# Rotary embedding over 16 heads: all rows on VectorE and GpSimd in groups of three, the first tile loaded ahead of the tables

## The chip, the cores and the metric

The kernel runs on one core of one Trainium2 chip. A core has TensorE (matrix multiply, writes to PSUM), VectorE (called DVE in the profile), ScalarE (ACT), GpSimd (POOL) and SyncE (SP), which here only issues transfers. Data is moved between the chip's memory and the on-chip SBUF by 16 DMA engines. The metric is the device time of one execution in microseconds (us), taken as the median of several runs.

## The reference

The input x is 16 x 512 x 1024 float32: batch, position, and 16 heads of 64 numbers. Each head's numbers are taken as two halves x1 and x2 of 32, and rotated with a cosine and a sine that depend on the position and on the place within the half:

```python
x = x.reshape(batch, seq, num_heads, head_dim)
x1, x2 = x[..., :half_dim], x[..., half_dim:]
cos, sin = cos[None, :, None, :], sin[None, :, None, :]
rotated = np.concatenate([x1 * cos - x2 * sin, x1 * sin + x2 * cos], axis=-1)
```

All is float32. x has 33.6 MB and so has the output: 67.1 MB must be moved. The tables cos and sin are 512 x 32 each, 64 KB.

## The kernel before, in words

**Tiling.** Two batch elements make one tile: 128 partitions, of which each holds R = 8 consecutive positions ("rows" of 1024 numbers), 32 KB a partition and 4 MB in all. There are NT = 8 tiles and NB = 5 buffers for them (pool `xin`). A tile is worked on in place and stored from where it was loaded.

**Tables.** The 64 partitions of `tabs` hold sin and cos once. A selection matrix `sel` (from `ident`, L75 to L83) and three matmuls (L88 to L90) spread them over 128 partitions in PSUM: `cos_ps`, and `sns_ps`, in which -sin and +sin lie side by side. ScalarE copies `sns_ps` to `sns` in SBUF (L94), since GpSimd reads it there. It also copies `cos_ps` to `cost` (L95), which nothing reads.

**Work on a tile** (`compute`). The output is x * cos + swap(x) * sns, where swap exchanges the halves of each head. The view `swapped` does the exchange in the access pattern, `cosb` and `snsb` repeat a table over the heads. Eight rows are divided in two ways:

- Rows 0 and 1 (`PEROWS`): the product swap(x) * sns is made by GpSimd for row 0 and by VectorE for row 1 (L121, tile `B`); VectorE multiplies x by cos in place (L131); TensorE adds the two by multiplying both with the identity into one PSUM tile `ps` (L136, L137, in halves of 512); ScalarE copies the sum back (L138).
- Rows 2 to 7 in three pairs (`PAIRS`): GpSimd makes T = swap(x) * sns (L126), VectorE makes pp = x * cos in PSUM (L142) and adds T and pp into x (L143).

`T` has two buffers, `pp` one. So GpSimd can be at most two groups ahead of VectorE.

**Order.** It is written out by hand (`manual_schedule`): each engine runs its instructions in the order of the program text. All transfers are issued by SP, in this order: sin, cos, the first tile in two halves (L63, L64), the loads of tiles 1 to 4 (L68), the stores of tiles 0 to 2 as each is done (L148), the loads of tiles 5 to 7, which each wait until a buffer has been stored (L68), the stores of tiles 3 and 4 (L152), of tiles 5 and 6 (L156), and tile 7 in two halves (L157, L158). A transfer that waits holds up those behind it on SP.

Of the kernel before, what the change touches and what calls it, by code (L numbers as in the profile page):

```python
# [7 lines left out]
FP32 = mybir.dt.float32  # L8
ALU = mybir.AluOpType


@with_exitstack
def kernel(
    ctx: ExitStack,
    tc: tile.TileContext,
    x: bass.AP,
    cos: bass.AP,
    sin: bass.AP,
    num_heads: bass.AP,
    out: bass.AP,  # L20
):
    nc = tc.nc
    P = nc.NUM_PARTITIONS
    batch, seq, dim = x.shape
    nh = num_heads
    hd = dim // nh
    half = hd // 2


    BP = 2  # L30
    HP = P // BP
    R = seq // HP
    NT = batch // BP
    assert HP * R == seq and BP * NT == batch
    NB = 5
    PAIRS = (2, 4, 6)
    PEROWS = (0, 1)

    xv = x.rearrange("b (p r) d -> (b p) (r d)", r=R)
    xv = xv.rearrange("(t p) f -> t p f", p=P)  # L40
    ov = out.rearrange("b (p r) h d -> (b p) (r h d)", r=R)
    ov = ov.rearrange("(t p) f -> t p f", p=P)
    cosv = cos.rearrange("(p r) j -> p (r j)", r=R)
    sinv = sin.rearrange("(p r) j -> p (r j)", r=R)

    fixed = ctx.enter_context(tc.tile_pool(name="fixed", bufs=1))
    xin = ctx.enter_context(tc.tile_pool(name="xin", bufs=NB))
    tpool = ctx.enter_context(tc.tile_pool(name="tpool", bufs=2))
    bpool = ctx.enter_context(tc.tile_pool(name="bpool", bufs=2))
    ptab = ctx.enter_context(tc.tile_pool(name="ptab", bufs=1, space=bass.MemoryType.PSUM))  # L50
    ppair = ctx.enter_context(tc.tile_pool(name="ppair", bufs=1, space=bass.MemoryType.PSUM))
    prow = ctx.enter_context(tc.tile_pool(name="prow", bufs=2, space=bass.MemoryType.PSUM))

    ctx.enter_context(tc.manual_schedule())


    tabs = fixed.tile([HP, 2, R * half], FP32, name="tabs")
    x_tiles = [None] * NT
    x_tiles[0] = xin.tile([P, R * dim], FP32, name="x_sb")
    H = R * dim // 2  # L60
    nc.sync.dma_start(out=tabs[:, 1], in_=sinv)
    nc.sync.dma_start(out=tabs[:, 0], in_=cosv)
    nc.sync.dma_start(out=x_tiles[0][:, :H], in_=xv[0][:, :H])  # L63
    nc.sync.dma_start(out=x_tiles[0][:, H:], in_=xv[0][:, H:])  # L64

    def load(t):
        x_tiles[t] = xin.tile([P, R * dim], FP32, name="x_sb")
        nc.sync.dma_start(out=x_tiles[t], in_=xv[t])  # L68

    for t in range(1, NB):  # L70
        load(t)


    ident = fixed.tile([P, P], FP32, name="ident")
    nc.gpsimd.memset(ident, 0.0)  # L75
    nc.gpsimd.affine_select(  # L76
        out=ident, in_=ident, compare_op=ALU.not_equal, fill=1.0,
        base=0, pattern=[[-1, P]], channel_multiplier=1,
    )
    sel = fixed.tile([HP, 2, P], FP32, name="sel")  # L80
    nc.vector.tensor_copy(out=sel[:, 0, :HP], in_=ident[:HP, :HP])  # L81
    nc.vector.tensor_copy(out=sel[:, 0, HP:], in_=ident[:HP, :HP])
    nc.vector.tensor_scalar_mul(out=sel[:, 1, :], in0=sel[:, 0, :], scalar1=-1.0)  # L83

    sns_ps = ptab.tile([P, R, 2, half], FP32, name="sns_ps")
    cos_ps = ptab.tile([P, R, half], FP32, name="cos_ps")
    sin3 = tabs[:, 1].rearrange("p (r j) -> p r j", r=R)
    nc.tensor.matmul(out=sns_ps[:, :, 1, :], lhsT=sel[:, 0, :], rhs=sin3, start=True, stop=True)  # L88
    nc.tensor.matmul(out=sns_ps[:, :, 0, :], lhsT=sel[:, 1, :], rhs=sin3, start=True, stop=True)  # L89
    nc.tensor.matmul(out=cos_ps.rearrange("p r j -> p (r j)"), lhsT=sel[:, 0, :], rhs=tabs[:, 0],  # L90
                     start=True, stop=True)
    sns = fixed.tile([P, R, 2, half], FP32, name="sns")
    cost = fixed.tile([P, R, half], FP32, name="cost")
    nc.scalar.copy(out=sns, in_=sns_ps)  # L94
    nc.scalar.copy(out=cost, in_=cos_ps)  # L95

    def view(ap, r0, n):

        return ap[:, r0 * dim:(r0 + n) * dim]

    def cosb(tab, r0, n):
        return bass.AP(tensor=tab.tensor, offset=tab.offset + r0 * half,
                       ap=[tab.ap[0], [half, n], [0, 2 * nh], [1, half]])

    def snsb(tab, r0, n):
        return bass.AP(tensor=tab.tensor, offset=tab.offset + r0 * hd,
                       ap=[tab.ap[0], [hd, n], [0, nh], [1, hd]])

    def swapped(xt, r0, n):
        return bass.AP(tensor=xt.tensor, offset=xt.offset + r0 * dim + half,  # L110
                       ap=[xt.ap[0], [hd, n * nh], [-half, 2], [1, half]])

    def compute(t):
        xt = x_tiles[t]
        ts = {}
        bs = {}

        for r in PEROWS:
            B = bpool.tile([P, dim], FP32, name="B")
            eng = nc.vector if r == PEROWS[-1] else nc.gpsimd  # L120
            eng.tensor_tensor(out=B, in0=swapped(xt, r, 1), in1=snsb(sns_ps if eng is nc.vector else sns, r, 1),  # L121
                              op=ALU.mult)
            bs[r] = B
        for r0 in PAIRS:
            T = tpool.tile([P, 2 * dim], FP32, name="T")
            nc.gpsimd.tensor_tensor(out=T, in0=swapped(xt, r0, 2), in1=snsb(sns, r0, 2), op=ALU.mult)  # L126
            ts[r0] = T

        for r in reversed(PEROWS):
            xr = view(xt, r, 1)  # L130
            nc.vector.tensor_tensor(out=xr, in0=xr, in1=cosb(cos_ps, r, 1), op=ALU.mult)  # L131
            for c in range(2):
                ps = prow.tile([P, dim // 2], FP32, name="ps")
                xc = xr[:, c * dim // 2:(c + 1) * dim // 2]
                bc = bs[r][:, c * dim // 2:(c + 1) * dim // 2]
                nc.tensor.matmul(out=ps, lhsT=ident, rhs=xc, start=True, stop=False)  # L136
                nc.tensor.matmul(out=ps, lhsT=ident, rhs=bc, start=False, stop=True)  # L137
                nc.scalar.copy(out=xc, in_=ps)  # L138
        for r0 in PAIRS:
            pp = ppair.tile([P, 2 * dim], FP32, name="pp")  # L140
            xr = view(xt, r0, 2)
            nc.vector.tensor_tensor(out=pp, in0=xr, in1=cosb(cos_ps, r0, 2), op=ALU.mult)  # L142
            nc.vector.tensor_tensor(out=xr, in0=ts[r0], in1=pp, op=ALU.add)  # L143

    for t in range(NB):
        compute(t)
        if t < NT - NB:
            nc.sync.dma_start(out=ov[t], in_=x_tiles[t])  # L148
    for t in range(NB, NT):
        load(t)  # L150
    for t in range(NT - NB, NB):
        nc.sync.dma_start(out=ov[t], in_=x_tiles[t])  # L152
    for t in range(NB, NT):
        compute(t)
        if t < NT - 1:
            nc.sync.dma_start(out=ov[t], in_=x_tiles[t])  # L156
    nc.sync.dma_start(out=ov[NT - 1][:, :H], in_=x_tiles[NT - 1][:, :H])  # L157
    nc.sync.dma_start(out=ov[NT - 1][:, H:], in_=x_tiles[NT - 1][:, H:])  # L158


# [33 lines left out]
```

## Time and profile before

| what | value |
|---|---|
| median of 3 runs | 164.61 us (164.56 to 164.94) |
| the profiled execution's own time | 164.86 us |
| its span, first to last instruction | 162.7 us |
| VectorE busy | 137.7 us (85%), 75 instructions |
| GpSimd busy | 127.1 us (78%), 38 instructions |
| TensorE matmul busy | 77.5 us (48%), 134 instructions |
| ScalarE busy | 21.0 us (13%), 35 instructions |
| moved by DMA | 67.25 MB, mean 413 GB/s |

The profile's page has the busy time of each engine, the span in 40 slices of 4.07 us (each digit is the busy share in tenths), the DMA queues with their packets, MB and share of the 16 engines' span, the costliest groups of instructions (line, engine, operation, out<-in with shapes, count | busy us, mean ns of one | idle us before them, and what ended most of that idle time), and the DMA issues (count, KB each, median us from issue to landing). The trace behind it can also be listed in order of time: start us, us, engine, line, operation, and in brackets the idle time before it and what ended it. SPq is SP's queue of issues.

### The profile page before, as it was taken

How to read it: one execution, taken by the hardware profiler on the slowest of the kernel's cores; microseconds unless marked ns; L12 is line 12 of the kernel's file. 1: busy time of each engine (PE TensorE's matmuls, PEld its weight loads, DVE VectorE, ACT ScalarE, POOL GpSimd, SP SyncE). 2: the span in 40 equal slices, each digit the busy share in tenths (PEclk: the TensorE clock that was granted, in tenths of full speed). 3: DMA queues.
4: the chain of work that ended last, by engine and by line, in shares of the span. 5: the costliest groups of instructions: out<-in, count | busy, mean ns of one | idle time of the engine just before them, and what ended most of it. 6: DMA issues, size and time to landing. Idle time of an engine off the chain costs nothing. (4 is left out here: it accounts for less than half of the span.)

```text
span 162.7 us, 575 instructions
## 1 busy us (share of the span) xinstructions
PE 77.5 (48%) x134; PEld 32.3 (20%) x134; DVE 137.7 (85%) x75; ACT 21.0 (13%) x35; POOL 127.1 (78%) x38
## 2 busy tenths in 40 slices
PE   2409910499019920894059701990089205990000
PEld 2204400243013400341024201330034002330000
DVE  1067999999999999999999999999999999999100
ACT  3200310013101210022002300121004100131000
POOL 1069999999998799959995999779995999590000
PEclk9999997559855995589557995699659975598555
DMA  4999989999899998999999999989989989999992
GB/s 101 387 447 467 435 387 500 403 395 508 387 403 371 443 459 387 475 427 403 467 413 411 467 411 427 475 387 459 443 387 459 443 387 492 411 411 415 439 427 121
DMA packets 2753, 67.25 MB, mean 413 GB/s; under 512 B 320, under 2 KB 448, under 8 KB 448
## 3 DMA queue, kind: packets, MB, share of 16 engines
q1 hardware_dynamic: 2752, 67.24, 97.0%
q14 instruction: 1, 0.01, 0.0%
HBM read 33.69 MB, written 33.55 MB: 413 GB/s over the span
## 5 line engine op out<-in xcount | busy, mean ns | idle before, releaser
L126 POOL TENSOR_TENSOR T<-x_sb,sns 128x2048 f32<-128x2048 f32 x24 | 108.3, 4532 | 10.4 <-DVE x_sb L143 10.4
L136 PE MATMUL ps<-x_sb,ident 128*128 128x512 f32 x64 | 44.4, 783 | 65.7 <-issue 41.4
L143 DVE TENSOR_TENSOR x_sb<-T,pp 128x2048 f32<-128x2048 f32 x24 | 54.9, 2287 | 3.4 <-POOL T L126 1.0
L142 DVE TENSOR_TENSOR pp<-x_sb,cos_ps 128x2048 f32<-128x2048 f32 x24 | 55.0, 2293 | 0.6
L137 PE MATMUL ps<-B,ident 128*128 128x512 f32 x64 | 40.1, 713 | 0.0
L138 ACT COPY x_sb<-ps 128x512 f32<-128x512 f32 x32 | 18.8, 586 | 121.7 <-PE ps L137 120.6
L136 PEld LDWEIGHTS ps<-x_sb,ident 128*128 128x128 f32 x64 | 15.1, 251 | 87.8 <-issue 81.0
L121 POOL TENSOR_TENSOR B<-x_sb,sns 128x1024 f32<-128x1024 f32 x8 | 18.8, 2350 | 8.3 <-DMA x_sb<-in_x_dram 8.3
L137 PEld LDWEIGHTS ps<-B,ident 128*128 128x128 f32 x64 | 15.4, 240 | 21.8 <-issue 21.8
L131 DVE TENSOR_TENSOR x_sb<-x_sb,cos_ps 128x1024 f32<-128x1024 f32 x16 | 18.8, 1218 | 0.5
L121 DVE TENSOR_TENSOR B<-x_sb,sns_ps 128x1024 f32<-128x1024 f32 x8 | 9.7, 1215 | 7.7 <-DMA x_sb<-in_x_dram 7.7
L88 PE MATMUL sns_ps<-tabs,sel 64*128 64x256 f32 x2 | 1.2, 696 | 3.1 <-DMA tabs<-in_sin_dram 3.1
L94 ACT ACT_TABLE_LOAD x1 | 1.3, 1283 | 0.7 <-PEq L175 0.7
L81 DVE COPY sel<-ident 64x64 f32<-64x64 f32 x1 | 0.2, 186 | 1.3 <-POOL ident L76 1.3
L88 PEld LDWEIGHTS sns_ps<-tabs,sel 64*128 64x128 f32 x2 | 0.5, 306 | 3.1 <-issue 3.1
L89 PE MATMUL sns_ps<-tabs,sel 64*128 64x256 f32 x2 | 1.1, 631 | 0.0
L90 PE MATMUL cos_ps<-tabs,sel 64*128 64x256 f32 x2 | 1.1, 631 | 0.0
L94 ACT COPY sns<-sns_ps 128x512 f32<-128x512 f32 x1 | 0.6, 586 | 3.2 <-PE sns_ps L89 3.2
L89 PEld LDWEIGHTS sns_ps<-tabs,sel 64*128 64x128 f32 x2 | 0.7, 333 | 0.2
L90 PEld LDWEIGHTS cos_ps<-tabs,sel 64*128 64x128 f32 x2 | 0.7, 333 | 0.2
L75 POOL MEMSET ident<- 128x128 f32 x1 | 0.2, 205 | 0.3 <-POOLq L175 0.3
L95 ACT COPY cost<-cos_ps 128x256 f32<-128x256 f32 x1 | 0.4, 373 | 0.3 <-PE cos_ps L90 0.3
(7 smaller groups left out, 1.1 us busy)
## 6 DMA issues: line engine op xcount, KB each, us to landing
x_sb<-in_x_dram SPq DMA_DIRECT2D x7, 4096.0 KB, 29.8
out_dram<-x_sb SPq DMA_DIRECT2D x7, 4096.0 KB, 27.5
x_sb<-in_x_dram SPq DMA_DIRECT2D x2, 2048.0 KB, 9.6
out_dram<-x_sb SPq DMA_DIRECT2D x2, 2048.0 KB, 10.1
tabs<-in_sin_dram SPq DMA_DIRECT2D x1, 64.0 KB, 2.2
tabs<-in_cos_dram SPq DMA_DIRECT2D x1, 64.0 KB, 2.3
```

What stands on the lines that cost most here:

```text
L88: nc.tensor.matmul(out=sns_ps[:, :, 1, :], lhsT=sel[:, 0, :], rhs=sin3, start=True, stop=True)
L89: nc.tensor.matmul(out=sns_ps[:, :, 0, :], lhsT=sel[:, 1, :], rhs=sin3, start=True, stop=True)
L90: nc.tensor.matmul(out=cos_ps.rearrange("p r j -> p (r j)"), lhsT=sel[:, 0, :], rhs=tabs[:, 0], start=True, stop=True)
L94: nc.scalar.copy(out=sns, in_=sns_ps)
L121: eng.tensor_tensor(out=B, in0=swapped(xt, r, 1), in1=snsb(sns_ps if eng is nc.vector else sns, r, 1), op=ALU.mult)
L126: nc.gpsimd.tensor_tensor(out=T, in0=swapped(xt, r0, 2), in1=snsb(sns, r0, 2), op=ALU.mult)
L131: nc.vector.tensor_tensor(out=xr, in0=xr, in1=cosb(cos_ps, r, 1), op=ALU.mult)
L136: nc.tensor.matmul(out=ps, lhsT=ident, rhs=xc, start=True, stop=False)
L137: nc.tensor.matmul(out=ps, lhsT=ident, rhs=bc, start=False, stop=True)
L138: nc.scalar.copy(out=xc, in_=ps)
L142: nc.vector.tensor_tensor(out=pp, in0=xr, in1=cosb(cos_ps, r0, 2), op=ALU.mult)
L143: nc.vector.tensor_tensor(out=xr, in0=ts[r0], in1=pp, op=ALU.add)
```

## The change

- TensorE and ScalarE no longer work on rows. `PEROWS`, `PAIRS`, the tiles `B` and `ps`, and lines L121 to L138 go.
- A tile is cut into groups of up to three rows, `MIDDLE` = rows 0-2, 3-5, 6-7. Each group has one GpSimd instruction (T), and two of VectorE (pp, and the sum), in this order in the program. `T` keeps two buffers and `pp` one, each now three rows long.
- The first tile is loaded in four pieces (rows 0, 1-2, 3-5, 6-7) that are also its groups (`FIRST`). The last tile has the groups 0-2, 3-4, 5-6, 7 (`LAST`) and is stored in these four pieces.
- The four pieces of the first tile are issued first on SP's queue. The tables are issued on ScalarE's queue.
- The copy to `cost` goes. There are 24 transfers where there were 20.

```diff
-    PAIRS = (2, 4, 6)
-    PEROWS = (0, 1)
+    FIRST = (0, 1, 3, 6, R)
+    MIDDLE = (0, 3, 6, R)
+    LAST = (0, 3, 5, 7, R)
+    G = 3
...
-    nc.sync.dma_start(out=tabs[:, 1], in_=sinv)
-    nc.sync.dma_start(out=tabs[:, 0], in_=cosv)
-    nc.sync.dma_start(out=x_tiles[0][:, :H], in_=xv[0][:, :H])
-    nc.sync.dma_start(out=x_tiles[0][:, H:], in_=xv[0][:, H:])
-
-    def load(t):
-        x_tiles[t] = xin.tile([P, R * dim], FP32, name="x_sb")
-        nc.sync.dma_start(out=x_tiles[t], in_=xv[t])
-
+    def load(t, cuts=(0, R)):
+        x_tiles[t] = xin.tile([P, R * dim], FP32, name="x_sb")
+        for a, b in zip(cuts, cuts[1:]):
+            nc.sync.dma_start(out=x_tiles[t][:, a * dim:b * dim], in_=xv[t][:, a * dim:b * dim])
+
+    def store(t, cuts=(0, R)):
+        for a, b in zip(cuts, cuts[1:]):
+            nc.sync.dma_start(out=ov[t][:, a * dim:b * dim], in_=x_tiles[t][:, a * dim:b * dim])
+
+    load(0, FIRST)
+    tabs = fixed.tile([HP, 2, R * half], FP32, name="tabs")
+    nc.scalar.dma_start(out=tabs[:, 1], in_=sinv)
+    nc.scalar.dma_start(out=tabs[:, 0], in_=cosv)
     for t in range(1, NB):
         load(t)
...
-    nc.scalar.copy(out=cost, in_=cos_ps)
...
-    def compute(t):
+    def compute(t, cuts):
         xt = x_tiles[t]
...
+        for a, b in zip(cuts, cuts[1:]):
+            n = b - a
+            xr = view(xt, a, n)
+            T = tpool.tile([P, G * dim], FP32, name="T")[:, :n * dim]
+            nc.gpsimd.tensor_tensor(out=T, in0=swapped(xt, a, n), in1=snsb(sns, a, n), op=ALU.mult)
+            pp = ppair.tile([P, G * dim], FP32, name="pp")[:, :n * dim]
+            nc.vector.tensor_tensor(out=pp, in0=xr, in1=cosb(cos_ps, a, n), op=ALU.mult)
+            nc.vector.tensor_tensor(out=xr, in0=T, in1=pp, op=ALU.add)

     for t in range(NB):
-        compute(t)
+        compute(t, FIRST if t == 0 else MIDDLE)
         if t < NT - NB:
-            nc.sync.dma_start(out=ov[t], in_=x_tiles[t])
+            store(t)
     for t in range(NB, NT):
         load(t)
     for t in range(NT - NB, NB):
-        nc.sync.dma_start(out=ov[t], in_=x_tiles[t])
+        store(t)
     for t in range(NB, NT):
-        compute(t)
...
+        compute(t, LAST if t == NT - 1 else MIDDLE)
+        store(t, LAST if t == NT - 1 else (0, R))
```

## The prediction, made before the changed kernel ran

> **What bounds the kernel now.** I read the page first (slices, queues), then the groups by shape, the time-ordered list of the first 12 us, of VectorE's steady part and of the last stores, and last the DMA issues with their landings.
>
> ```profile
> span 162.7 us, 575 instructions
> DVE  1067999999999999999999999999999999999100
> POOL 1069999999998799959995999779995999590000
> DMA  4999989999899998999999999989989989999992
> q1 hardware_dynamic: 2752, 67.24, 97.0%
> ```
>
> The DMA row is full from the second slice to the last but one: the 16 engines work 97.0% of 162.7 = 157.8 us on 67.24 MB, 426 GB/s. VectorE stops three slices before the end: only transfers run in the last 11 us. So the kernel is bound by its transfers, and it can gain only at the front, where the DMA starts late, or lose at the end, if the last result comes too late for the last store.
>
> ```profile
> 0.73 0.54 SPq L61 DMA_DIRECT2D tabs<-in_sin_dram  x1
> 1.33 0.57 SPq L62 DMA_DIRECT2D tabs<-in_cos_dram  x1
> 1.96 0.58 SPq L63 DMA_DIRECT2D x_sb<-in_x_dram  x1
> 3.11 1.19 PE L88 MATMUL sns_ps<-tabs,sel 64*128 64x256 f32 x2 [3.11 <-DMA tabs<-in_sin_dram]
> 5.19 0.59 ACT L94 COPY sns<-sns_ps 128x512 f32<-128x512 f32 x1 [3.17 <-PE sns_ps L89]
> 9.60 2.35 POOL L121 TENSOR_TENSOR B<-x_sb,sns 128x1024 f32<-128x1024 f32 x1 [8.29 <-DMA x_sb<-in_x_dram]
> ...
> 146.89 0.33 SPq L157 DMA_DIRECT2D out_dram<-x_sb  x1
> 151.29 0.33 SPq L158 DMA_DIRECT2D out_dram<-x_sb  x1
> ```
>
> The sines are ready for GpSimd at 5.19 + 0.59 = 5.8, but its first work waits for the 2 MB half of tile 0 until 9.60. The first x transfer is issued third, at 1.96. At the end, VectorE lets the last half go at 151.29.
>
> ```profile
> L126 POOL TENSOR_TENSOR T<-x_sb,sns 128x2048 f32<-128x2048 f32 x24 | 108.3, 4532 | 10.4 <-DVE x_sb L143 10.4
> L142 DVE TENSOR_TENSOR pp<-x_sb,cos_ps 128x2048 f32<-128x2048 f32 x24 | 55.0, 2293 | 0.6
> L143 DVE TENSOR_TENSOR x_sb<-T,pp 128x2048 f32<-128x2048 f32 x24 | 54.9, 2287 | 3.4 <-POOL T L126 1.0
> L131 DVE TENSOR_TENSOR x_sb<-x_sb,cos_ps 128x1024 f32<-128x1024 f32 x16 | 18.8, 1218 | 0.5
> L121 POOL TENSOR_TENSOR B<-x_sb,sns 128x1024 f32<-128x1024 f32 x8 | 18.8, 2350 | 8.3 <-DMA x_sb<-in_x_dram 8.3
> ```
>
> ```profile
> 18.79 2.29 DVE L142 TENSOR_TENSOR pp<-x_sb,cos_ps 128x2048 f32<-128x2048 f32 x1
> 21.18 2.29 DVE L143 TENSOR_TENSOR x_sb<-T,pp 128x2048 f32<-128x2048 f32 x1
> 23.51 2.29 DVE L142 TENSOR_TENSOR pp<-x_sb,cos_ps 128x2048 f32<-128x2048 f32 x1
> ```
>
> A two-row pair on VectorE repeats every 23.51 - 18.79 = 4.72 us (2.29 twice, 0.10 before the add, 0.03 after it). A tile now costs VectorE 17.56 (its first instructions of tiles 1 and 2 stand at 28.11 and 45.67).
>
> ```profile
> out_dram<-x_sb SPq DMA_DIRECT2D x2, 2048.0 KB, 10.1
> tabs<-in_sin_dram SPq DMA_DIRECT2D x1, 64.0 KB, 2.2
> ```
>
> The two last stores landed 9.8 and 10.3 us after their issues (by the view of each line), the last at 151.29 + 10.3 = 161.6. From there to the end of the span are 1.1 us, and the execution's own time, 164.86, has 2.2 outside the span. That time is 0.25 above the median of the runs (164.61, from 164.56 to 164.94); I make the sum against 164.86 and do not take the 0.25 off.
>
> **The change, part by part.**
>
> *Removed.* 128 matmuls, 32 ScalarE copies and the cost copy go. None stood on the path: ScalarE's copies waited 120.6 us for TensorE, and both are idle for half of the span. Worth 0.
>
> *GpSimd.* Slope from one row to two: 4.532 - 2.350 = 2.18 us a row, so three rows take 6.71, and 6.69 from start to start (two-row ones repeat every 13.49 / 3 = 4.50, the one-row one every 2.30). A tile of 3 + 3 + 2 rows: 17.9, before 2.30 + 13.49 = 15.8.
>
> *VectorE.* Slope 2.293 - 1.218 = 1.07 a row: three rows take 3.36, a three-row pair 4.72 + 2 x 1.07 = 6.86. A tile: 2 x 6.86 + 4.72 = 18.43, which is 0.87 more than now. VectorE is slower than GpSimd's 17.9, so it paces every tile but the first. The form of its operands stays: one in SBUF, one in PSUM. So I keep the slopes, without a charge for the two engines meeting.
>
> *First tile.* Let P0 be GpSimd's start on row 0. One row ends at P0 + 2.35, two at P0 + 6.83, the three at P0 + 13.51. VectorE has only to add there, and is paced by GpSimd: it adds the three rows from P0 + 13.54 to P0 + 16.9, does the last two rows in 4.72, and is free at P0 + 21.65. GpSimd stays ahead from then on; its two T buffers come free at least 0.6 us before VectorE would starve. Six tiles: 6 x 18.43 = 110.58. The last one, 3 + 2 + 2 + 1 rows: 6.86 + 2 x 4.72 + 2.54 = 18.84. VectorE ends at **P0 + 151.07**.
>
> *P0.* Row 0 (0.5 MB) is issued at 0.73 and should land by about 5: its issue, 1.3 until bytes flow, 1.2 of data, and a slow first packet. So not it but the sines set P0. Sin and cos are issued on ScalarE's queue at 0.73 and 1.33 (0.54 and 0.57 each); the table load behind them (1.28) ends near 3.2, well before the copy of sns, so it costs nothing. In the trace sin lands 2.2 us after its issue, with no other transfer about; TensorE starts at 3.11 and sns is ready at 5.8. Now x flows on the same engines. Low end: sin is not delayed, P0 = 5.85. High end: it waits out row 0, 1.2 us at 426 GB/s and some 0.7 of start-up: P0 = 7.75. I take the middle of the two, 6.7, because sin and row 0 are issued at the same moment and neither end is nearer in the trace. Cos has no such weight: VectorE's first product has slack until T of row 0 is there, 2.35 later.
>
> Here a rule speaks against the change. The Trainium skill, DMA: Bandwidth & Descriptors, section Queues, rings and completion order, says that each DMA engine serves its queues in turn and empties a whole packet of typically 9 to 17 descriptors before it switches. Row 0's 8 rows on each engine would then all go ahead of sin, P0 would be 5.85 + 1.2 = 7.05 and the sum below 164.75 instead of 164.4. No row of this trace shows two queues at once.
>
> *SP.* The four pieces of tile 0 take the time of the four issues that stood there (to about 3.1), so loads 1 and 2 are issued as before. As compiled, loads 3 and 4 wait until sin and row 0 have landed, about 5; loads 1 and 2, 2 x 9.8 us of transfer, cover that. Behind it the order of stores and loads is unchanged.
>
> *Stores.* Before, store 6 came to move near 141.2 (the next half landed at 156.7, less 4.9 of its own data, less 9.8, less about 0.8 to land). The front moves the stream 1.23 forward (1.96 to 0.73) and the tables' 0.13 MB, 0.3 us, back into it: 140.3. Store 6 is issued at P0 + 132.2 = 138.9 and flows from 140.2: just covered. The pieces of tile 7 are issued at 145.8, 150.5, 155.2 and 157.8; the stream would want them at 150, 153.8, 156.2 and 158.7, and they can flow 1.3 after issue. The first two are covered, the third is late by 0.3, and the last sets the end.
>
> *Last store.* Nothing of before shows 0.5 MB stored on an idle queue. Low: the 64 KB table landed in 2.2, so 0.5 MB in 2.2 + 0.44 MB / 426 GB/s = 3.3. High: the first half of tile 0 landed 7.5 after its issue, of which 4.9 are its data: 2.6 + 1.2 = 3.8. I take 3.3; a 64 KB transfer is the nearest row in size, and the half was issued behind the tables.
>
> **Sum**: 6.7 + 151.07 = 157.8; 0.05 to SP's issue; 3.3 to land: 161.1, against 161.6; 1.1 to the span's end; 2.2 outside: **164.4**. Equal to P0 + 157.7. That is 0.5 under the profiled 164.86 and 0.2 under the median: the bound passes from the transfers alone to VectorE's chain, and what the front gains the extra 0.87 us a tile takes away.
>
> **The rivals.**
>
> *Faster: the transfers keep the bound.* If P0 is near 5.85, VectorE ends at 156.9 and its chain gives 163.55, less than the transfers allow. These start 1.23 earlier and take the tables' 0.3 and nothing else: 164.86 - 0.9 = 163.95. For it: sin's packets are few and short. Against it: VectorE's last store pieces would have to come without any of the waits above. It holds from P0 under about 6.3.
>
> *Slower: the tables starve behind x.* Sin and cos are 64 rows of 1 KB that share engines with a queue of x. If sin waits out rows 0 to 2 (1.5 MB, 3.7 us, and 0.7 of start-up), P0 = 10.2 and the time 167.9; if only row 0 and the last store's high price, 165.9. Each us of P0 is a us at the end, since VectorE never idles after tile 0. It decides from P0 over 7.4 (165.1). For it: a queue that was alone now meets a full one. Against it: sin is issued as early as row 0.
>
> *Not as told: GpSimd paces.* If VectorE's three-row instructions cost less than the slope, GpSimd's chain ends at P0 + 143.2 and VectorE's last row 4 us later: 6.7 + 147.5 leaves the transfers as the bound, 163.95 again. The rows of one and two rows, equal to 0.01 us in every tile, speak against it.
>
> **How the numbers follow.** A difference of 0.3% (0.5 us) is about what a measurement of this kernel can tell from none; against the median that means under 164.12 or over 165.10. VectorE's chain with P0 from 6.3 to 7.4: 0.50, own range 164.0 to 165.1, of which 0.06 is under 164.12. Transfers keep the bound, by either road: 0.27, all faster. Tables or last store late: 0.23, slower. So faster 0.33, within 0.44, slower 0.23. The range leaves out 0.2: from 163.7, the transfers' price less half of the spread of the runs, to 165.7, which takes in row 0 waited out whole, with a little of the last store's high price.
>
> **What the profile after would show.** GpSimd's first 128x1024 starts at 6.7 (5.85 to 7.75), released by ScalarE's sns and not by a DMA; T of 128x3072 takes 6.71, VectorE's 128x3072 3.36; VectorE's tiles repeat every 18.43 and it ends at 157.8 without idling after tile 0; the last store is issued then and lands 3.3 later; the DMA row has gaps only in the last two or three slices. I am wrong if three rows cost more than the slope, if sin lands after 5, if the DMA row shows gaps in the middle, or if the last 0.5 MB takes 4 us or more.

## The result, and the profile after

| | before | changed |
|---|---|---|
| median | 164.61 us | 164.12 us (7 runs, 163.94 to 164.34) |
| ratio to before | | 0.9963, 95% interval 0.9946 to 0.998 |
| the profiled execution's own time | 164.86 | 164.05 |
| span | 162.7 | 162.3 |
| VectorE busy | 137.7 (85%) | 145.3 (90%) |
| GpSimd busy | 127.1 (78%) | 143.4 (88%) |

The change makes the kernel 0.5 us faster. Forecast were 164.4 and "within 0.3%" as the likeliest of three; the median lies just on the border between that and "faster". A second comparison, with more runs of the kernel before beside it, gave 0.9945 (0.9926 to 0.9964), which is clearly on the faster side.

The page of the changed kernel:

```profile
span 162.3 us, 229 instructions
DVE  1069979999999999999999999999999999999991
POOL 1099999999999999999899998999899998999800
DMA  5999998999999998998998999999999999699996
q1 hardware_dynamic: 3168, 67.11, 97.1%
q10 hardware_dynamic: 160, 0.13, 0.3%
```

Before, VectorE stopped three slices ahead of the end and the DMA row was full. Now VectorE's row is full up to the last slice and the DMA row has a 6 in the slice from 138 to 142 us. q10 is the new second queue with the two tables. The start, in order of time:

```profile
0.73 0.53 ACTq L71 DMA_DIRECT2D tabs<-in_sin_dram  x1
0.73 5.00 SPq L63 DMA_DIRECT2D x_sb<-in_x_dram  x8
5.05 1.19 PE L91 MATMUL sns_ps<-tabs,sel 64*128 64x256 f32 x2 [5.05 <-DMA tabs<-in_sin_dram]
7.12 0.59 ACT L96 COPY sns<-sns_ps 128x512 f32<-128x512 f32 x1 [3.90 <-PE sns_ps L92]
7.79 13.45 POOL L120 TENSOR_TENSOR T<-x_sb,sns 128x1024 f32<-128x1024 f32 x3 [6.49 <-ACT sns L96]
9.36 1.23 DVE L122 TENSOR_TENSOR pp<-x_sb,cos_ps 128x1024 f32<-128x1024 f32 x1 [7.48 <-PE cos_ps L93]
```

x and sin are issued at the same moment, 0.73. TensorE waits for sin until 5.05 where it was 3.11, so GpSimd starts at P0 = 7.79: earlier than the 9.60 of before, later than the 6.7 that I took. The groups with their shapes kept apart, and the end:

```profile
L120 POOL TENSOR_TENSOR T<-x_sb,sns 128x3072 f32<-128x3072 f32 x14 | 93.4, 6701 | 2.8 <-DVE x_sb L123 2.8
L122 DVE TENSOR_TENSOR pp<-x_sb,cos_ps 128x3072 f32<-128x3072 f32 x14 | 47.1, 3362 | 0.5
L123 DVE TENSOR_TENSOR x_sb<-T,pp 128x3072 f32<-128x3072 f32 x14 | 47.0, 3355 | 2.3 <-POOL T L120 1.0
```

```profile
29.39 3.36 DVE L122 TENSOR_TENSOR pp<-x_sb,cos_ps 128x3072 f32<-128x3072 f32 x1
47.82 3.36 DVE L122 TENSOR_TENSOR pp<-x_sb,cos_ps 128x3072 f32<-128x3072 f32 x1
...
139.94 19.20 SPq L67 DMA_DIRECT2D out_dram<-x_sb  x5
...
157.56 1.22 DVE L123 TENSOR_TENSOR x_sb<-T,pp 128x1024 f32<-128x1024 f32 x1
```

Three rows cost what the slope said (6.70 on GpSimd, 3.36 on VectorE), and a tile 47.82 - 29.39 = 18.43 us. Store 6 is issued at 139.94, when tile 6 is done. Just there the transfers have run dry. In the busy time by stretches (the two last columns are the DMA share and GB/s):

```profile
139.00:140.00 1.00, 0.00 (x0) 0.00 (x0) 0.96 (x2) 0.00 (x0) 1.00 (x1) 1.00 0.08 33
```

Before, in the same microsecond:

```profile
139.00:140.00 1.00, 1.00 (x3) 0.48 (x2) 0.90 (x2) 0.02 (x1) 1.00 (x1) 0.50 1.21 524
```

The last store, from the DMA issues:

```profile
out_dram<-x_sb SPq DMA_DIRECT2D x1, 512.0 KB, 2.6
```

VectorE ends at 157.56 + 1.22 = 158.78, the store is issued at 158.81 and lands 2.6 later at 161.4, where before the last one landed at 161.6. It did not find the engines idle:

```profile
158.00:159.00 1.00, 0.00 (x0) 0.00 (x0) 0.78 (x1) 0.00 (x0) 0.00 (x0) 1.00 1.03 418
```

By the trace's packets (the single transfers of one DMA engine) the piece ahead of it, issued at 156.22, moves from 157.05 to 159.6 on most engines, and the last piece from 159.66 to 161.1.

### The profile page after: what moved, and what is told of

Read it like the earlier page. It is cut to its first block, busy times and chain, and to the rows that moved or that the text cites. A ratio compares the mean times of both kernels' runs of the same rounds, so it can differ in the third digit from the quotient of the medians.

```text
span 162.3 us, 229 instructions
## 1 busy us (share of the span) xinstructions
PE 3.3 (2%) x6; PEld 1.7 (1%) x6; DVE 145.3 (90%) x55; ACT 1.9 (1%) x2; POOL 143.4 (88%) x32
## 4 chain that ended last, share of the span: by engine, by line
DVE 79%; DMA 7%; POOL 7%; issue 2%; POOLq 1%; SPq 1%; DVEq 0%
DVE x_sb L123 41%; DVE pp L122 38%; DMA x_sb<-in_x_dram 7%; POOL T L120 7%; POOLq L166 1%; SPq L63 1%; DVEq L123 0%; POOLq L120 0%
## 5 line engine op out<-in xcount | busy, mean ns | idle before, releaser
L120 POOL TENSOR_TENSOR T<-x_sb,sns 128x3072 f32<-128x3072 f32 (+2 forms) x26 | 142.7, 5537 | 9.9 <-ACT sns L96 6.5
L122 DVE TENSOR_TENSOR pp<-x_sb,cos_ps 128x3072 f32<-128x3072 f32 (+2 forms) x26 | 72.5, 2787 | 8.3 <-PE cos_ps L93 7.5
L123 DVE TENSOR_TENSOR x_sb<-T,pp 128x3072 f32<-128x3072 f32 (+2 forms) x26 | 72.3, 2780 | 3.8 <-POOL T L120 1.3
```

The lines of the kernel that those rows point to most:

```text
L120: nc.gpsimd.tensor_tensor(out=T, in0=swapped(xt, a, n), in1=snsb(sns, a, n), op=ALU.mult)
L122: nc.vector.tensor_tensor(out=pp, in0=xr, in1=cosb(cos_ps, a, n), op=ALU.mult)
L123: nc.vector.tensor_tensor(out=xr, in0=T, in1=pp, op=ALU.add)
```

## The experiments

Two theories. **A**: the changed kernel is bound by VectorE's chain, P0 + 151; the transfers alone would end earlier. **B**: the transfers bind it as they bound the kernel before, and the gain is that x starts earlier. The ratios are to the kernel before, on the same chip; its median there was 165.0 to 165.1.

| run | ratio (95%) | median |
|---|---|---|
| front only | 0.9892 (0.9871 to 0.9913) | 163.35 |
| work only | 1.0063 (1.0041 to 1.0085) | 166.16 |
| tables first | 0.9974 (0.9958 to 0.999) | 164.67 |
| less VectorE work | 0.9876 (0.9851 to 0.9901) | 162.95 |
| row 0 in halves | 0.9961 (0.994 to 0.9983) | 164.46 |
| tables behind row 0 | 0.9976 (0.9954 to 0.9998) | 164.73 |
| idle work | 0.9937 (0.9914 to 0.9961) | 164.20 |
| late x | 1.0025 (1.0005 to 1.0045) | 165.53 |
| changed, again | 0.9945 (0.9926 to 0.9964) | 164.08 |
| front only, again | 0.9899 (0.988 to 0.9918) | 163.32 |
| row 7 on TensorE | 1.0904 (1.0883 to 1.0925) | 179.98 |
| last tile in halves | 1.0174 (1.0152 to 1.0196) | 167.90 |

**The front alone.** The kernel before with x first and the tables on ScalarE's queue:

```diff
...
-    nc.sync.dma_start(out=tabs[:, 1], in_=sinv)
-    nc.sync.dma_start(out=tabs[:, 0], in_=cosv)
-    nc.sync.dma_start(out=x_tiles[0][:, :H], in_=xv[0][:, :H])
-    nc.sync.dma_start(out=x_tiles[0][:, H:], in_=xv[0][:, H:])
+    FRONT = (0, 1, 2, 4, 6, R)
+    for a, z in zip(FRONT, FRONT[1:]):
+        nc.sync.dma_start(out=x_tiles[0][:, a * dim:z * dim], in_=xv[0][:, a * dim:z * dim])
...
+    nc.scalar.dma_start(out=tabs[:, 1], in_=sinv)
+    nc.scalar.dma_start(out=tabs[:, 0], in_=cosv)
```

> The kernel before with only the front of the change: the first tile is issued on SP first (in pieces of rows 0, 1, 2-3, 4-5, 6-7) and the tables on ScalarE's queue; the work on the rows stays with four engines. Theory A (in the changed kernel VectorE's chain, P0 + 151, sets the end; the transfers alone would end earlier): here VectorE needs 17.56 a tile and ends near 150, the stream starts 1.2 earlier than before and never runs dry, so 163.3 to 163.8, faster than the changed kernel. Theory B (the transfers set the end in the changed kernel as well, and its gain is the front's): the same time as the changed kernel, 164.1. Store 6 should be issued before 134 and the DMA show no gap near 139.

Measured 163.35, as A said. From its page, and its last VectorE instruction:

```profile
DMA  5999999999999999999999999999999999999993
```

```profile
147.08 2.29 DVE L144 TENSOR_TENSOR x_sb<-T,pp 128x2048 f32<-128x2048 f32 x1
```

The DMA row has no hole, and VectorE is done 12 us before the end. The front alone gains 1.7 us, more than the whole change. It changes three things at once: the order, the queue of the tables, and the cut of tile 0 into five pieces.

**The work alone.** The changed kernel with the front of before:

```diff
-    load(0, FIRST)
     tabs = fixed.tile([HP, 2, R * half], FP32, name="tabs")
-    nc.scalar.dma_start(out=tabs[:, 1], in_=sinv)
-    nc.scalar.dma_start(out=tabs[:, 0], in_=cosv)
+    nc.sync.dma_start(out=tabs[:, 1], in_=sinv)
+    nc.sync.dma_start(out=tabs[:, 0], in_=cosv)
+    load(0, (0, R // 2, R))
```

> The changed kernel with the front of before: sin and cos first on SP, then tile 0 in halves; groups of three rows and the last store in four pieces stay. Theory A: GpSimd starts at 9.6 as before, VectorE ends at 9.6 + 151.0 = 160.6, the last store lands 2.6 later, 163.2, and with 0.9 to the end of the span and 1.75 outside of it the time is 165.9. Theory B: the stream is the one of before, so 164.6.

Measured 166.16; A said 165.9, B 164.6. In its list by time:

```profile
9.67 53.44 POOL L120 TENSOR_TENSOR T<-x_sb,sns 128x1024 f32<-128x1024 f32 x10 [8.36 <-DMA x_sb<-in_x_dram]
```

```profile
159.43 1.22 DVE L123 TENSOR_TENSOR x_sb<-T,pp 128x1024 f32<-128x1024 f32 x1
```

P0 is 9.67 and VectorE ends at 160.65, 150.98 later; in the changed kernel the two are 158.78 - 7.79 = 150.99 apart. A later start comes out at the end one for one. The work on rows by itself loses 1.1 us. The parts add up roughly: -1.7 + 1.1 = -0.6, and the change measured -0.5 and, in the second comparison, -1.0. In that comparison the work loses 0.8 once the front is in place (164.08 against the 163.32 of the front alone).

**The tables first**, with the four pieces of tile 0 behind them on SP:

```diff
-    load(0, FIRST)
     tabs = fixed.tile([HP, 2, R * half], FP32, name="tabs")
-    nc.scalar.dma_start(out=tabs[:, 1], in_=sinv)
-    nc.scalar.dma_start(out=tabs[:, 0], in_=cosv)
+    nc.sync.dma_start(out=tabs[:, 1], in_=sinv)
+    nc.sync.dma_start(out=tabs[:, 0], in_=cosv)
+    load(0, FIRST)
```

> The changed kernel with the tables on SP's queue ahead of the four pieces of tile 0. Sin should land near 2.9 again and GpSimd start at 5.9 instead of 7.79. Theory A: the chain ends at 5.9 + 151.0 = 156.9 and would give 162.2; the stream starts about 1.1 later than in the changed kernel and its 1.3 us gap near 139 closes, so 163.0 to 163.8: faster than the changed kernel although x starts later. Theory B (what counts is how early x starts): 164.1 + 1.1 = 165.2.

```profile
6.14 18.04 POOL L120 TENSOR_TENSOR T<-x_sb,sns 128x1024 f32<-128x1024 f32 x4 [4.84 <-DMA x_sb<-in_x_dram]
```

```profile
DMA  3999989999999999999999999999999999999993
```

GpSimd starts at 6.14, VectorE ends at 157.24, and the hole in the DMA row has closed. Yet the time is 164.67, between the two forecasts. Here the transfers bind, and they end later than I had worked out; the two runs on the tables behind row 0 and on late x look for the reason.

**Less for VectorE.** Row 7 of tiles 1 to 6 is not added, so the kernel leaves out a part of the result; all else stays, the transfers too:

```diff
-            nc.vector.tensor_tensor(out=xr, in0=T, in1=pp, op=ALU.add)
+            k = n - 1 if 0 < t < NT - 1 and b == R else n
+            nc.vector.tensor_tensor(out=view(xt, a, k), in0=T[:, :k * dim], in1=pp[:, :k * dim], op=ALU.add)
```

> The changed kernel with the addition left out for row 7 of tiles 1 to 6: the third group's add of VectorE is one row instead of two, 1.07 us less a tile, 6.4 us in all; all else stays. Theory A: VectorE ends near 152.4, the gap near 139 goes, and the time falls to what the transfers allow, 162.4 to 163.6. Theory B: no change, 164.1.

```profile
153.15 1.22 DVE L124 TENSOR_TENSOR x_sb<-T,pp 128x1024 f32<-128x1024 f32 x1
```

```profile
DMA  5999999999999999999999999999999999999994
```

VectorE ends at 154.37 (GpSimd paces now, so 4.4 and not 6.4 earlier), the hole is gone, and the time falls to 162.95. B is out: with the same transfers the changed kernel could be 1.1 us faster, and VectorE's chain keeps it from that. The tables-first run and this one are both bound by their transfers and load tile 0 in the same four pieces; they differ by 1.7 us. So it is the order and the queue that gain, and not the cut.

**Row 0 in halves**, to see what sin waits for:

```diff
...
-    load(0, FIRST)
+    load(0, (0, 0.5) + FIRST[1:])
```

> The changed kernel with row 0 of the first tile loaded in two halves of 256 KB (25 transfers). Theory A1 (a DMA engine takes turns between the two queues by whole transfers, so sin lands with the first transfer on SP's queue and cos with the second): sin lands 0.6 earlier than in the changed kernel, 3.6 us after its issue instead of 4.2, cos with the second half near 4.9 instead of 8.1, GpSimd starts at 7.2 instead of 7.79, VectorE ends 0.6 earlier, the gap of the DMA near 139 shrinks by that and the time is 0.6 under the changed kernel's, a ratio of 0.9925 to 0.993 to the kernel before where the changed kernel has 0.9963. Rival A2 (a fixed price of the second queue): sin at 4.2, GpSimd at 7.8, no change.

```profile
7.19 2.34 POOL L120 TENSOR_TENSOR T<-x_sb,sns 128x1024 f32<-128x1024 f32 x1 [5.89 <-ACT sns L96]
9.91 15.61 POOL L120 TENSOR_TENSOR T<-x_sb,sns 128x2048 f32<-128x2048 f32 x3 [0.38 <-DMA x_sb<-in_x_dram]
```

Sin lands 3.6 us after its issue and P0 is 7.19, to the tenth what A1 said. By the trace's packets, sin's start from 2.65 to 3.51 here, between the two halves, and from 3.46 to 4.09 in the changed kernel, between row 0 and rows 1-2. So the engines take turns between the queues by whole transfers of this size. This fits what the Trainium skill has in DMA: Bandwidth & Descriptors, section Queues, rings and completion order: a whole packet of descriptors is drained before the switch.

The time missed the forecast: 164.46 is 0.4 above the changed kernel on the same chip (164.08) and not 0.6 below it. The profile tells only a part of why, and its execution was the longest of the 12 (165.25). In it one DMA engine fell behind in the first tile: it ended rows 1-2 at 9.5, the other 15 by 8.1. GpSimd waited for them (the second line) and VectorE ended only 0.2 earlier. Cos landed at 6.9, where 4.9 was expected; half of its packets had begun by 4.2, behind the second half of row 0. What held the other executions back stays open.

**The tables behind row 0, and x late.** Both ask why the tables-first run lost more than its later start. The first has all transfers on SP, in the order row 0, sin, cos, rows 1-2 and so on; the second lets x wait for the sines:

```diff
...
+    x_tiles[0] = xin.tile([P, R * dim], FP32, name="x_sb")
+    for i, (a, b) in enumerate(zip(FIRST, FIRST[1:])):
+        nc.sync.dma_start(out=x_tiles[0][:, a * dim:b * dim], in_=xv[0][:, a * dim:b * dim])
+        if i == 0:
+            nc.sync.dma_start(out=tabs[:, 1], in_=sinv)
+            nc.sync.dma_start(out=tabs[:, 0], in_=cosv)
```

> The changed kernel with all transfers on SP's queue: row 0, sin, cos, then the other pieces of tile 0. Sin is issued near 1.3 and lands near 4, GpSimd starts near 6.9, VectorE ends near 157.9. The question is the 0.7 to 0.9 us that packets lose between 50 and 53 us in the kernel before and with the tables first, and not in the changed kernel. If it comes with the tables on SP's queue, it is here too; if it comes with a late start of x, it is not here. Without it the time is 0.6 to 0.9 under the changed kernel's (ratio 0.991 to 0.993), as VectorE's chain starts 0.9 earlier; with it the transfers bind and the ratio is 0.995 to 0.997.

```diff
...
     nc.scalar.dma_start(out=tabs[:, 0], in_=cosv)
+    x_tiles[0] = xin.tile([P, R * dim], FP32, name="x_sb")
+    nc.vector.tensor_copy(out=x_tiles[0][:HP, 0:1], in_=tabs[:, 1, 0:1])
+    for a, b in zip(FIRST, FIRST[1:]):
+        nc.sync.dma_start(out=x_tiles[0][:, a * dim:b * dim], in_=xv[0][:, a * dim:b * dim])
```

> The changed kernel, tables on ScalarE's queue, but the first load of x waits until VectorE has copied one number out of the landed sines: x starts some 2.5 us later. GpSimd starts near 7 to 7.5, so VectorE's chain is hardly later or earlier than in the changed kernel; the stream binds: 1.3 of the delay goes into the gap near 139, the rest, 1.2, comes out, a ratio near 1.003. If packets lose 0.7 to 0.9 us between 50 and 53 us here too, that loss goes with the late start of x (ratio 1.007); if not, with the tables on SP's queue.

The 32 KB packets that begin between 45 and 55 us, from one trace of each kernel (the steady value is 1213 ns; the excess is the sum over it, for one engine):

```
kernel                first x packet   mean ns   longest   excess us
before                     3.18          1309      2018      0.77
work only                  3.18          1320      1952      0.84
tables first               3.18          1337      2065      0.96
tables behind row 0        1.76          1386      2575      1.24
late x                     4.08          1334      2100      0.89
changed                    1.75          1222      1601      0.07
front only                 1.82          1227      1535      0.11
less VectorE work          1.76          1224      1474      0.09
row 0 in halves            1.74          1224      1495      0.09
idle work                  1.73          1236      1567      0.19
```

The loss of 0.8 to 1.2 us sits in the last packets of tile 4's load, ahead of the first store. It comes with the tables on SP's queue (tables behind row 0: x starts early and it is there) and also with a late x and the tables on ScalarE's queue. So neither of my two conditions is the cause; only with both the early x and the second queue is it absent. In the run with row 7 on TensorE, told of below, it is absent here and comes at two later switches between loads and stores (0.9 after 80 us, 0.8 after 110). A second trace of the changed kernel and of the front alone has 0.05 and 0.03. What the loss is stays open. With it the tables-first run is accounted for: the forecast's upper end plus 0.9 is 164.7. The run with the tables behind row 0 was slower than the changed kernel (164.73 against 164.08) for another reason as well: sin landed 3.8 us after its issue, GpSimd started at 7.88 and not at 6.9. The ratio of the late x, 1.0025, is the forecast's first case although the loss is there; the sum for it was off by that much.

**Idle work.** 64 matmuls and 32 ScalarE copies whose results nobody reads:

```diff
...
+        for i in range(4):
+            for j in range(2):
+                nc.tensor.matmul(out=flat(sns_ps), lhsT=ident, rhs=flat(sns), start=j == 0, stop=j == 1)
+            nc.scalar.copy(out=sink, in_=flat(sns_ps))
```

> The changed kernel with 64 matmuls and 32 ScalarE copies that nothing waits for (identity by sns into sns_ps, copied to a tile that nobody reads); they run in the first third. They stand for the instructions that the change removed. If these instructions are free, as I said, the time is the changed kernel's and the execution's own time stays 1.75 above the span. If the 0.4 us by which the changed kernel's own time stands closer to its span comes from the two engines' instructions, it is 2.1 to 2.2 above the span here and the time 0.4 more (ratio 0.9985).

Measured 164.20, where the changed kernel measures 164.08 to 164.12, and its own time, 164.25, stands 1.78 above its span of 162.47, as in the changed kernel. So these instructions of the two engines are free as such. They are half of the matmuls and all of the row copies that the change took out, without the waits that those had.

**Three more on one chip**: the changed kernel and the front alone again, and the changed kernel with row 7 of tiles 1 to 6 added by TensorE.

> The changed kernel again, beside the next three on one chip: ratio 0.995 to 0.998 to the kernel before, VectorE's end near 158.8, the last store landed 2.6 after its issue.

> The kernel before with the front of the change alone, again: ratio 0.987 to 0.992, 0.8 to 1.2 us under the changed kernel on this chip.

```diff
...
+            if 0 < t < NT - 1 and b == R:
+                n = n - 1
+                last = view(xt, b - 1, 1)
+                nc.vector.tensor_tensor(out=last, in0=last, in1=cosb(cos_ps, b - 1, 1), op=ALU.mult)
+                for c in range(2):
+                    lo, hi = c * dim // 2, (c + 1) * dim // 2
+                    nc.tensor.matmul(out=ps, lhsT=ident, rhs=last[:, lo:hi], start=True, stop=False)
+                    nc.tensor.matmul(out=ps, lhsT=ident, rhs=T[:, n * dim + lo:n * dim + hi], start=False, stop=True)
+                    nc.scalar.copy(out=last[:, lo:hi], in_=ps)
...
```

> The changed kernel with row 7 of tiles 1 to 6 added by TensorE and copied back by ScalarE, as rows 0 and 1 were before (sums through the bank of sns_ps): VectorE needs 0.9 less a tile and ends near 155. If VectorE's chain was what the changed kernel lost on, the gap near 139 closes and the ratio is 0.987 to 0.990, as with the addition left out; if that chain did not bind, the changed kernel's ratio. If the 0.3 to 0.4 us between the span and the execution's own time belong to work of TensorE up to the end, its own time is 2.1 above the span; if not, 1.8.

The first two came as expected: 164.08 and 163.32. The third is a plain miss, 180. Its waits show why:

```profile
POOL T L121 <- PE sns_ps L129: 16.5, 6, 3.1
DVE x_sb L134 <- POOL T L121: 13.2, 8, 2.5
```

TensorE reads T, so T's buffer is held until its sum is done. In tile 1 that takes from 44.76 to 53 us: 7.5 us are TensorE's eight matmul instructions, 0.7 its wait until the first half is copied out of the one PSUM tile `ps`. GpSimd has two T buffers and waits six times, 16.5 us in all, for one of them; VectorE waits for GpSimd in turn. I had moved work off VectorE and put a longer hold on what feeds it. In the kernel before, TensorE reads a buffer of its own (`B`), so that its sums do not hold T.

**The last tile in halves.**

```diff
-        store(t, LAST if t == NT - 1 else (0, R))
+        store(t, (0, R // 2, R) if t == NT - 1 else (0, R))
```

> The changed kernel with the last tile stored in two halves instead of four pieces. The second half (2 MB) is issued when VectorE ends, 158.8, and lands 2.6 + 1.5 MB / 426 GB/s = 6.3 later, at 165.1 instead of 161.4: 3.7 us more, ratio 1.019. If the stream rather than VectorE set the end, the cut would be worth little. If the own time stands 2.1 above the span instead of 1.8, that difference goes with the size of the last store.

```profile
158.86 0.33 SPq L67 DMA_DIRECT2D out_dram<-x_sb  x1
```

```profile
out_dram<-x_sb SPq DMA_DIRECT2D x2, 2048.0 KB, 6.3
```

6.3 us to land, and 167.90, 3.8 over the changed kernel: what is issued when VectorE ends is the end. Here the first half had left the engines by 157.5, and the second began to move at 159.69, 0.83 us after its issue. The cut of the last tile is worth 3.8 us here, and without it the change would be slower.

**The version that beats both** is the front alone, 163.32 to 163.35. Its intervals (up to 0.9913 and 0.9918) lie below those of the changed kernel (from 0.9946 and 0.9926).

## Why the prediction was right

By its own steps:

- *What binds.* Right: VectorE's chain took the place of the transfers. Less VectorE work (-1.1 us) and the later start (+2.1) show it from both sides.
- *Costs of the work.* Right to 0.02 us for each instruction; 18.43 a tile; VectorE ends P0 + 150.99 against 151.07.
- *P0.* The term that was most off: 6.7 taken, 7.79 measured, just past the high end of 7.75. I took the middle because no row told between the ends. The high end was the right one: sin waits out the whole of row 0 and its start-up. P0's 1.1 us came out at VectorE's end in full. The rule of the Trainium skill (DMA: Bandwidth & Descriptors, section Queues, rings and completion order), which stood beside the sum, named the mechanism; 7.05 by it was too low since it left out the start-up of 0.7.
- *Last store.* 3.3 taken, 2.6 measured, outside 3.3 to 3.8. -0.7. The 64 KB table is not the floor that I made of it. From issue to the first packet the table took 1.3, the store 0.85, and 0.83 in the run with halves, where the engines were idle; its data took 1.45, and it landed 0.3 after its last packet. The store did not find the engines idle, as its price had it: they were on the piece ahead of it until 159.6, just when it could begin. So a smaller last piece alone would have had to wait for the piece ahead of it; no run tries one.
- *The ends.* From the last landing to the span's end 0.9 instead of 1.1, outside the span 1.78 instead of 2.2. -0.6. Sum: VectorE's end 1.0 later than forecast, so 164.4 + 1.0 - 0.7 - 0.6 = 164.1; the profiled execution took 164.05.
- *Store 6 "just covered".* Wrong: the transfers ran dry for 1.3 us near 139. P0 made the store 1.0 late, and the stream came about 0.9 early; 0.7 of this are the slow packets near 50 us, which were in its pace before and were gone. It cost nothing, since the chain and not the stream set the end. With this the DMA row has a gap ahead of its last three slices, one of the signs that the prediction gave for being wrong; sin landed at 4.9, just inside another of them (5).
- *Removed work, worth 0.* The idle work bears it out, as far as it goes.
- *Rivals.* The transfers' price of 163.95 was too high: front alone 163.35, less VectorE work 162.95 on a chip on which the kernel before is 0.45 slower. I counted the earlier start and not the slow packets. The slow case's condition, P0 over 7.4, came true, and did not make it slower because the last store and the ends gave the same amount back. In the rival in which GpSimd paces, 143.2 + 4 is 147.2 and not 147.5; where GpSimd did pace, with less VectorE work, VectorE ended at P0 + 146.5. The mechanism was right, but that the sum came within 0.3 us was luck: errors of opposite sign, P0 on one side, the last store and the ends on the other. And "within 0.3%", which had the highest chance (0.44), is on the border in the first comparison and missed in the second, where "faster" (0.33) is what was measured.

## What to carry to other kernels

A kernel that its transfers bind has two places to gain, the first and the last microseconds. Here the order and the queue of the first transfers are together worth 1.7 us, and doing the work on fewer engines lost 0.8 of it again: with 0.87 us more in each of six tiles and some 3 us more in the first, VectorE ended 7.5 us later than before, although it began earlier, and no longer ahead of the stream. Where the compute ends last, cut the last store small: what is issued at the end lands at the end (6.3 us later with 2 MB, 2.6 with 0.5 MB).

A small transfer on a second queue waited here for the transfer that was being served on the first: the 64 KB of sin landed 4.2 us after its issue beside 512 KB, 3.6 beside 256 KB, 2.2 ahead of them. If something depends on the small one, what goes ahead of it should be small; that this shortens the whole kernel no run here shows.

## What the runs showed that I had not expected

- The last packets of the last load before the first store take up to 2.0 to 2.6 us instead of 1.21 in five kernels, 0.8 to 1.2 us for each engine, and hardly there in the others. The condition is open.
- In kernels whose transfers bind, one of the 16 engines ends 0.5 to 1.3 us after the others (before: 15 engines by 160.3, one at 161.2; less VectorE work: 159.1 and 159.9). The hole near 139 swallows this lag in the changed kernel: ahead of the hole 15 engines end by 139.7 and one at 140.9, and at the end all 16 end together (160.94 to 161.1).
- The own time stands 1.78 or 1.79 us above the span in all kernels whose rows VectorE and GpSimd alone finish, and 1.9 to 2.2 above it in the four profiles where TensorE and ScalarE work on rows up to the last or last but one tile. Neither the instructions as such (idle work: 1.78) nor the size of the last store (halves: 1.79) makes the difference; its cause was not tested further.
